# A decoder layer in float32: the sums of eight weight blocks and one rstd product, moved in the order of the instructions

## The chip, the cores and the metric

The kernel runs on one core of one Trainium2 chip. The core has five engines that run beside each other and are tied by semaphores: TensorE (PE in the profile, its weight loads are PEld), VectorE (DVE), ScalarE (ACT), GpSimd (POOL) and SyncE (SP). Here POOL and SP do little but issue transfers. Each engine works through its own instructions in one order that is fixed when the kernel is built. The metric is the device time of one execution in microseconds (us); lower is better.

## The reference

One layer of a hybrid decoder on 256 tokens of 2048 features, all in float32. What is computed:

```
h = rms_norm(x, g_mix);  z = h @ w_in
y = concat(pool_mixer(z_pool), mla(z_q, z_kv, z_kr), memory_attention(z_mq, mem)) @ w_o
x = x + y
h2 = rms_norm(x, g_ffn)
g = h2 @ w_gate;  gc = conv_b + conv_w[0]*g[t-2] + conv_w[1]*g[t-1] + conv_w[2]*g[t]
x = x + (silu(gc) * (h2 @ w_up)) @ w_down
```

The feed-forward width is 5632, so w_gate and w_up are cut into 44 tiles of 128 columns each, and w_down into 44 rows of blocks, taken in pairs.

## The kernel before, in words

**Products.** Each float32 weight block comes from memory into a staging tile `wr` (8 KB for each of 128 partitions, three buffers). ScalarE rounds half of it to a high part `wh` (line 102), VectorE subtracts to get the low part `wl` (line 103); each has four buffers. TensorE then makes three products: high by high, high by low, low by high. The out-projection takes its activations as the stationary operand (`gemm_n`, lines 184 to 186, 512 columns, results in `psm`); the first gate and up tile use `gemm_t` (line 133), the other 43 use `gemm_pair` (line 168).

**The out-projection** is 16 calls of `out_part`, counted from 0. The first eight take the activations of the pooling and memory branches (`catm`, part of `cat`), with the steps of the eight attention heads between their products; the last eight take those of the MLA heads, two for each of the four column blocks n. One part loads one block of `w_o` and splits it in two halves of 12 products each. After the second part of a column block `out_add` (line 804) adds the product to `x1n`, ScalarE squares it (line 830) and POOL stores it to `x1s` (line 831). `turn(n)` transposes a finished block on TensorE (line 837) and splits the result into `h2`, tile `h`: ScalarE makes the high half (line 196), VectorE the low half (line 197). In the stream of TensorE `turn(n - 1)` stands behind the two parts of block n, so `turn(2)` stands at the end of the out-projection.

**The jobs.** The down-projection at the end of the layer saves products by working on differences of weight blocks. For some block rows those differences are made far ahead and parked in memory: a job loads one block row of `w_down` into a tile `wk` (`job_load`, line 757, on POOL's queue), makes four differences in place (`job_sums`, line 764, VectorE) and writes them to `tsum` in two stores (line 766, POOL's queue). The first eight jobs run during the out-projection with two buffers for `wk`; the others run in the feed-forward stage with tiles `wj`. `first_jobs`, called at the end of each part, runs the next job if the part's number is in the table `FIRST` (line 768), and then starts the load for the job after the next, into the buffer that has just been stored. So a load waits until both stores of the job two before it have landed.

**The first gate tile** is begun early: `gemm_t` on features 0 to 1023 for gate and up (line 913), then `turn(3)` for the last column block, then `x1_rstd` (line 915), then `gemm_t` on features 1024 to 2047 for gate and up (line 919). `x1_rstd` sums the squares, takes the root on ScalarE (line 211), inverts it on VectorE, makes two diagonal matrices `tok` (line 857) and multiplies them by a matrix of ones (line 859), so that `r1` holds the rstd of each token on all partitions (copy on line 860, ScalarE). `r1` is first needed by `glu(0)` (line 871), which runs in the middle of gate tile 1. Block 3 of `h2` is needed by the last four of the eight k steps of the second half.

**What sets the order.** The kernel is written as one program; a scheduler spreads it over the engines by its own costs. `keep` marks instructions that are to be taken in the order of the program; the others may be moved more freely. The products of the parts numbered over 8 and the splits are not marked. The order that comes out is the one that counts; it is shown below where the change touches it.

Of the kernel before, what the change touches and what calls it, by code (L numbers as in the profile page):

```python
# [22 lines left out]
KD = D // P  # L23
# [14 lines left out]
HS = 1024  # L38
# [26 lines left out]
def layer(ctx, tc, xT_d, xn_d, memT_d, vec_d, tab_d, w_z_d, w_mqkr_d, w_q_d, w_kv_d, w_mem_d, w_pool_d, w_o_d,  # L65
# [14 lines left out]
    def ps_main():  # L80
        return psm.tile([P, 512], F32, tag="m", name=nm("psm"))

    def ps_aux():
        return psa.tile([P, 512], F32, tag="a", name=nm("psa"))

    def load_w(src, n, cut=STG, kept=False):
        raw = stage.tile([P, STG], F32, tag="wr", name=nm("wr"), bufs=3)
        for c in range(0, n, cut):
            keep(nc.sync.dma_start(raw[:, c:min(n, c + cut)], src[:, c:min(n, c + cut)]), kept)
        return raw[:]  # L90
# [5 lines left out]
    def split_w(raw, o, n, cut=HS, kept=False, shift=0):  # L96

        hi = stage.tile([P, HS + 64], F32R, tag="wh", name=nm("wh"), bufs=4)[:, shift:shift + HS]
        lo = stage.tile([P, HS + 64], F32R, tag="wl", name=nm("wl"), bufs=4)[:, shift:shift + HS]
        for c in range(0, n, cut):  # L100
            e = min(n, c + cut)
            keep(nc.scalar.copy(hi[:, c:e], raw[:, o + c:o + e]), kept)  # L102
            keep(nc.vector.tensor_tensor(lo[:, c:e], raw[:, o + c:o + e], hi[:, c:e].bitcast(F32), op=ALU.subtract),  # L103
                 kept)
        return hi, lo
# [7 lines left out]
    def rounds(act, k, low):  # L113

        m = act(k)
        h, l = (m[:, 0], m[:, 1]) if len(m.shape) == 3 else (m[:, 0:T], m[:, T:2 * T])
        return (h,) if low else (h, l)

    def gemm_t(ps, raw, o, act, ks, first=True, last=True, between=None):


        ks = list(ks)
        nk = HS // P
        cs = range(0, len(ks), nk)
        for c in cs:
            kc = ks[c:c + nk]

            parts = split_w(raw, o + c * P, len(kc) * P, shift=16 if c // nk % 2 else 48)
            lows = (False, True) if c // nk % 2 == 0 else (True, False)
            for low in lows:  # L130
                for i, k in enumerate(kc):
                    for a, m in enumerate(rounds(act, k, low)):
                        nc.tensor.matmul(ps, parts[low][:, i * P:(i + 1) * P], m,  # L133
                                         start=first and c + i + a == 0 and not low,
                                         stop=last and c == cs[-1] and i == len(kc) - 1 and low == lows[1],
                                         skip_group_check=True)
            if between is not None and c == 0:
                between()
# [70 lines left out]
    def rsqrt_(dst, src, scale):  # L209

        nc.scalar.activation(dst, src, AF.Sqrt, bias=eps[:], scale=scale)
        nc.vector.reciprocal(dst, dst)
# [22 lines left out]
    def tok():  # L235
        return mp.tile([P, 512], F32, tag="tok", name=nm("tok"), bufs=3)
# [79 lines left out]
    ps = ps_aux()  # L316
# [24 lines left out]
    pss = [[ps_main()[:] for _ in range(2)] for _ in range(NT)]  # L341
    for c in range(KD // 2):
        raw = raw0 if c == 0 else load_w(w_mem_d[c], STG, HS if c == 1 else STG)
# [16 lines left out]
    ps = ps_aux()  # L360
# [61 lines left out]
    pss = [[ps_aux()[:, :NH] for _ in range(2)] for _ in range(NT)]  # L422
    for c in range(KD // 2):
        raw = load_w(w_mqkr_d[c], 2 * 576)
# [41 lines left out]
    class Head:  # L466
# [23 lines left out]
        def turn(self):  # L490
            tp = ps_aux()
            for x, (k, i) in enumerate(self.blocks):
                a = self.spans[i][0]
                keep(nc.tensor.transpose(tp[:, x * P:(x + 1) * P], self.p[:, a + k * P:a + (k + 1) * P], identf[:]))
            self.pT = mp.tile([P, 512], F32, tag="pT", name=nm("pT"), bufs=2)
            nb = len(self.blocks) * P
            nc.scalar.copy(self.pT[:, :nb], tp[:, :nb])
# [37 lines left out]
    for m in range(6):  # L535
        raw = load_w(w_z_d[m], STG)
        if m in (1, 3):
            keep(nc.sync.dma_start(x1n[:, m // 2, :], xn_d[m // 2]))
        ps = ps_main()[:, 0:T]
# [212 lines left out]
    def job_place():  # L752
        return fp.tile([P, STG], F32, tag="wj", name=nm("wj"), bufs=2)[:]

    def job_load(i, raw):

        keep(nc.gpsimd.dma_start(raw, w_dn_d[SUMMED[i]]))
        return i, raw

    def job_sums(i, raw):  # L760

        r = raw.rearrange("p (b n) -> p b n", n=NN)
        for d, a, b in ((1, 0, 1), (0, 2, 0), (2, 2, 1), (3, 3, 2)):
            keep(nc.vector.tensor_tensor(r[:, d], r[:, a], r[:, b], op=ALU.subtract))  # L764
        for h in range(2):
            keep(nc.gpsimd.dma_start(tsum[:, i, h * HS:(h + 1) * HS], raw[:, h * HS:(h + 1) * HS]))  # L766

    FIRST = (1, 2, 4, 6, 8, 9, 11, 13)

    def first_load(i):  # L770
        return job_load(i, mp.tile([P, STG], F32, tag=("xgt", "zl")[i % 2], name=nm("wk"))[:])
# [4 lines left out]
    def first_jobs():  # L776

        if parts[0] in FIRST:
            i, raw = waiting.pop(0)
            job_sums(i, raw)  # L780
            if i + 2 < len(FIRST):
                waiting.append(first_load(i + 2))
# [23 lines left out]
    pss = {}  # L806
# [33 lines left out]
    for n in range(4):  # L840
        pss = [[ps_main()[:]] for _ in range(NT)]
# [10 lines left out]
    def x1_rstd():  # L852
        nc.vector.tensor_reduce(rc[:], ssx[:], axis=AX.X, op=ALU.add)
        rsqrt_(rc[:], rc[:], 1.0 / D)
        dg = tok()
        for tt in range(NT):
            nc.vector.tensor_scalar(dg[:, tt * P:(tt + 1) * P], identf[:], rc[:, tt:tt + 1], None, op0=ALU.mult)
        ps = ps_aux()
        nc.tensor.matmul(ps[:, 0:T], ones[:], dg[:, 0:T], start=True, stop=True)
        nc.scalar.copy(r1[:], ps[:, 0:T])  # L860
# [49 lines left out]
    raws = [load_w(w[0], STG) for w in (w_g_d, w_u_d)]  # L910
    pss = [ps_main()[:, 0:T] for _ in range(2)]
    for ps, raw in zip(pss, raws):
        gemm_t(ps, raw, 0, h2, range(8), last=False)
    turn(3)
    x1_rstd()
    mix.close()
    fp = ctx.enter_context(tc.tile_pool(name="ffn", bufs=1))
    for ps, raw in zip(pss, raws):
        gemm_t(ps, raw, HS, h2, range(8, KD), first=False)
    job = job_load(len(FIRST), job_place())  # L920
    late = len(SUMMED) - len(FIRST)
    job_at = {1 + i * (KF - 7) // (late - 1): len(FIRST) + i for i in range(late)}
    for f in range(1, KF):
        rows = [load_w(w[f], STG, kept=True) for w in (w_g_d, w_u_d)]
        behind = (lambda p=pss: glu(0, *p)) if f == 1 else None
        pss = [ps_main()[:, 0:T] for _ in range(2)]
# [220 lines left out]
```

## Time and profile before

| | |
|---|---|
| three runs | 996.36, 997.23 and 997.76 us; median 997.23 us |
| the profiled execution | 996.85 us, of which 995.1 us lie between its first and last instruction (the span) |
| busy: PE, PEld, DVE, ACT, POOL | 986.6, 912.9, 784.1, 577.7, 67.1 us |
| granted TensorE clock | 0.999 of full speed |
| transfers | 294.88 MB, 296 GB/s on average |

In the rows below a line of the timeline reads: start in us from the beginning of the span, length in us, engine, line of the kernel, operation, tile written <- tiles read, how many, and in brackets how long the engine stood before it and what released it. Several instructions of one kind in a row are merged into one line. Numbers at the end of a tile's name are left out in the profile, and stand in the order of the instructions.

### The profile page before, as it was taken

The page shows a single profiled execution, that of the slowest core. Times are in us where ns is not written, and L with a number is a line of the kernel's source. Part 1 is how long each engine was busy: PE and PEld are TensorE (multiplying, and loading weights), DVE is VectorE, ACT ScalarE, POOL GpSimd, SP SyncE. Part 2 cuts the span into 40 slices and gives each one's busy share as a digit, 9 for nine tenths or more (in the row PEclk, how much of TensorE's full clock was granted, in tenths as well). Part 3 has the DMA queues.
Part 4 walks back from the last instruction along what each step waited for, and adds up shares of the span by engine and source line. Part 5 has one row for each costly group of instructions (what it writes and reads, how often), then busy time and mean ns, then how long its engine had stood idle before and what let it go on. Part 6 is the DMA issues. An engine that isn't in the chain of part 4 may idle for free.

```text
span 995.1 us, 17312 instructions
## 1 busy us (share of the span) xinstructions
PE 986.6 (99%) x6870; PEld 912.9 (92%) x6870; DVE 784.1 (79%) x1174; ACT 577.7 (58%) x779; POOL 67.1 (7%) x130
## 2 busy tenths in 40 slices
PE   9999999999999999999999999999999999999998
PEld 8899988888879999999999999999999888888886
DVE  6878588977677788767868877777876889899987
ACT  6777665644466555455555545555454666847763
POOL 1100000110210101000000100000000000000000
PEclk9999999999999999999999999999999999999999
DMA  9867446696798977888877788879897999999992
GB/s 360 295 244 287 137 160 221 233 323 239 295 323 316 349 283 273 310 291 294 292 298 275 276 293 312 307 264 333 307 354 259 343 396 356 370 340 391 368 388 100
DMA packets 50577, 294.88 MB, mean 296 GB/s; under 512 B 5696, under 2 KB 6208, under 8 KB 25024
## 3 DMA queue, kind: packets, MB, share of 16 engines
q1 hardware_dynamic: 33696, 213.16, 58.8%
q0 software_dynamic: 16368, 79.83, 21.5%
q8 instruction: 54, 0.88, 0.3%
q10 hardware_dynamic: 432, 0.79, 0.2%
q14 instruction: 27, 0.22, 0.1%
HBM read 255.61 MB, written 38.14 MB: 295 GB/s over the span
## 4 chain that ended last, share of the span: by engine, by line
PE 94%; DVE 2%; DMA 1%; ACT 1%; issue 1%; POOL 0%; DVEq 0%; POOLq 0%
PE psm L168 47%; PE psm L184 4%; PE psm L185 4%; PE psm L186 4%; PE psm L149 4%; PE psa L958 4%; PE psa L957 4%; PE psa L956 4%; PE psm L958 4%; PE psm L957 4%; PE psm L956 4%; PE psm L133 2%; PE psa L722 1%; DMA wk<-in_w_dn 1%; PE psa L184 1%; PE psa L186 1%
## 5 line engine op out<-in xcount | busy, mean ns | idle before, releaser
L103 DVE TENSOR_TENSOR wl<-wr,wh 128x1024 fp32r<-128x1024 f32 (+2 forms) x344 | 397.1, 1162 | 135.7 <-ACT wh L102 121.8
L102 ACT CAST wh<-wr 128x1024 fp32r<-128x1024 f32 (+2 forms) x344 | 343.0, 1002 | 183.8 <-PE psm L168 87.5
L168 PE MATMUL psm<-h,wh 128*128 128x256 f32 x2752 | 319.1, 276 | 0.0
L168 PEld LDWEIGHTS psm<-h,wh 128*128 128x128 f32 x2752 | 315.3, 188 | 0.0
L168 PE MATMUL psm<-h,wl 128*128 128x256 f32 x1376 | 162.9, 276 | 0.0
L168 PEld LDWEIGHTS psm<-h,wl 128*128 128x128 f32 x1376 | 159.2, 188 | 0.0
L873 ACT ACTIVATE gc<-g,vec 128x256 f32<-128x256 f32 x44 | 26.5, 603 | 73.0 <-DVE g L871 73.0
L102 ACT CAST wh<-wj 128x1024 fp32r<-128x1024 f32 (+1 forms) x48 | 47.1, 982 | 22.0 <-PE psa L957 11.6
L103 DVE TENSOR_TENSOR wl<-wj,wh 128x1024 fp32r<-128x1024 f32 (+1 forms) x48 | 53.7, 1132 | 6.3 <-ACT wh L102 2.4
L764 DVE TENSOR_TENSOR wj<-wj 128x512 f32<-128x512 f32 x80 | 55.0, 687 | 1.0
L876 ACT ACTIVATE gc<-gc 128x256 f32<-128x256 f32 x44 | 18.4, 417 | 59.6 <-DVE gc L875 59.6
L875 DVE SCALAR_TENSOR_TENSOR gc<-g,vec,gc 128x255 f32<-128x255 f32 x88 | 42.3, 481 | 1.5
L103 DVE TENSOR_TENSOR wl<-dn,wh 128x1024 fp32r<-128x1024 f32 (+1 forms) x36 | 40.1, 1133 | 3.4 <-ACT wh L102 1.7
L102 ACT CAST wh<-dn 128x1024 fp32r<-128x1024 f32 (+1 forms) x36 | 35.4, 983 | 10.7 <-PE psm L957 4.9
L186 PE MATMUL psm<-wl,cat 128*128 128x512 f32 x96 | 37.6, 391 | 1.5 <-DVE wl L103 1.5
L766 POOL DMA_DIRECT2D tsum<-wj x40 | 21.4, 534 | 257.9 <-DVE s L896 166.1
L184 PE MATMUL psm<-wh,cat 128*128 128x512 f32 x96 | 38.1, 397 | 0.0
L185 PE MATMUL psm<-wh,cat 128*128 128x512 f32 x96 | 37.4, 389 | 0.0
L957 PE MATMUL psm<-wh,aS 128*128 128x512 f32 x84 | 32.7, 389 | 0.0
L957 PE MATMUL psa<-wh,aS 128*128 128x512 f32 x84 | 32.7, 389 | 0.0
L956 PE MATMUL psm<-wh,aS 128*128 128x512 f32 x84 | 32.7, 389 | 0.0
L956 PE MATMUL psa<-wh,aS 128*128 128x512 f32 x84 | 32.7, 389 | 0.0
(251 smaller groups left out, 1486.4 us busy)
## 6 DMA issues: line engine op xcount, KB each, us to landing
wr<-in_w_g SPq DMA_DIRECT2D x44, 1024.0 KB, 6.4
wr<-in_w_u SPq DMA_DIRECT2D x44, 1024.0 KB, 6.2
wj<-in_w_dn POOLq DMA_DIRECT2D x20, 1024.0 KB, 5.8
tsum<-wj POOLq DMA_DIRECT2D x40, 512.0 KB, 6.7
wr<-in_w_o SPq DMA_DIRECT2D x16, 1024.0 KB, 5.5
wr<-in_w_dn SPq DMA_DIRECT2D x16, 768.0 KB, 6.6
wr<-tsum SPq DMA_DIRECT2D x12, 1024.0 KB, 6.8
wj<-tsum SPq DMA_DIRECT2D x12, 1024.0 KB, 7.0
```

The lines of the kernel that those rows point to most:

```text
L102: keep(nc.scalar.copy(hi[:, c:e], raw[:, o + c:o + e]), kept)
L103: keep(nc.vector.tensor_tensor(lo[:, c:e], raw[:, o + c:o + e], hi[:, c:e].bitcast(F32), op=ALU.subtract), kept)
L149: keep(nc.tensor.matmul(ps, parts[k // nk][low][:, i * P:(i + 1) * P], m, start=k + a == 0 and low == low_first, stop=k == KD - 1 and low ...
L168: nc.tensor.matmul(ps, parts[k // nk][low][:, i * P:(i + 1) * P], m, start=k + a == 0 and low == (s == 1), stop=k == KD - 1 and low == (s ...
L184: keep(nc.tensor.matmul(ps, xh, hi[:, i, o], start=first and i == 0, stop=False), kept)
L185: keep(nc.tensor.matmul(ps, xl, hi[:, i, o], start=False, stop=False), kept)
L186: keep(nc.tensor.matmul(ps, xh, lo[:, i, o], start=False, stop=last and i == nk - 1), kept)
L764: keep(nc.vector.tensor_tensor(r[:, d], r[:, a], r[:, b], op=ALU.subtract))
L875: nc.vector.scalar_tensor_tensor(gc[:, d:T], g[:, 0:T - d], v(w, f), gc[:, d:T], op0=ALU.mult, op1=ALU.add)
L956: nc.tensor.matmul(ps, a[0], b[0], start=first, stop=False)
L957: nc.tensor.matmul(ps, a[1], b[0], start=False, stop=False)
L958: nc.tensor.matmul(ps, a[0], b[1], start=False, stop=last)
```

## The change

Two edits. The table of the parts behind which the eight jobs' sums run is another one, and in the first gate tile `x1_rstd` moves from ahead of the second half of gate and up to the place between them. `mix.close()` and the opening of the next pool, which free and take the memory of the tiles of the first stages, come after these products instead of ahead of them. No instruction is added or taken away.

```diff
-    FIRST = (1, 2, 4, 6, 8, 9, 11, 13)
+    FIRST = (1, 3, 4, 6, 7, 9, 10, 12)
...
     turn(3)
-    x1_rstd()
+    for i, (ps, raw) in enumerate(zip(pss, raws)):
+        gemm_t(ps, raw, HS, h2, range(8, KD), first=False)
+        if i == 0:
+            x1_rstd()
     mix.close()
     fp = ctx.enter_context(tc.tile_pool(name="ffn", bufs=1))
-    for ps, raw in zip(pss, raws):
-        gemm_t(ps, raw, HS, h2, range(8, KD), first=False)
```

The second job runs one part later; the fifth, seventh and eighth run one part earlier. Three places show what this makes of the order.

POOL's queue from the load for the fifth job (`wk_2398`) on; the load for the seventh is `wk_2645` before and `wk_2587` after, the load for the eighth is `wk_2687` in both. Before:

```order
L757 DMA wk_2398<-in_w_dn 128x2048
L766 DMA tsum<-wk_2260 128x1024 x2
L757 DMA wk_2534<-in_w_dn 128x2048
L766 DMA tsum<-wk_2398 128x1024 x2
L831 DMA x1s<-x1n 128x512 x2
L757 DMA wk_2645<-in_w_dn 128x2048
L766 DMA tsum<-wk_2534 128x1024 x2
L766 DMA tsum<-wk_2645 128x1024
L757 DMA wk_2687<-in_w_dn 128x2048
```

The same queue after:

```order
L757 DMA wk_2398<-in_w_dn 128x2048
L766 DMA tsum<-wk_2324 128x1024 x2
L757 DMA wk_2534<-in_w_dn 128x2048
L766 DMA tsum<-wk_2398 128x1024 x2
L757 DMA wk_2587<-in_w_dn 128x2048
L766 DMA tsum<-wk_2534 128x1024 x2
L757 DMA wk_2687<-in_w_dn 128x2048
L831 DMA x1s<-x1n 128x512 x2
L766 DMA tsum<-wk_2587 128x1024 x2
```

The last two loads have moved ahead: the seventh job's is no longer behind stores of `x1s`, the eighth job's stands ahead of the first of them. On VectorE, before, the sums of the sixth job (`wk_2534`, behind the splits of part 9) stand ahead of those of the fifth (`wk_2398`, behind the splits of part 10); after, those of the fifth begin just ahead of the splits of part 8, and those of the sixth keep their place.

VectorE in parts 12 and 13, where the sums are those of the seventh job before and of the eighth after; `wl_2840` and `wl_2856` before, `wl_2846` and `wl_2862` after, are the splits for the two halves of part 13. Before:

```order
L103 TENSOR_TENSOR wl_2822<-wr_2803,wh_2821 128x1024
L764 TENSOR_TENSOR wk_2645<-wk_2645 128x512
L103 TENSOR_TENSOR wl_2840<-wr_2837,wh_2839 128x1024
L764 TENSOR_TENSOR wk_2645<-wk_2645 128x512
L804 TENSOR_TENSOR x1n<-x1n,psm_2697 128x512
L764 TENSOR_TENSOR wk_2645<-wk_2645 128x512
L804 TENSOR_TENSOR x1n<-x1n,psm_2698 128x512
L764 TENSOR_TENSOR wk_2645<-wk_2645 128x512
L197 SCALAR_TENSOR_TENSOR h_2584<-psa_2781,vec,h_2584 128x256
L197 SCALAR_TENSOR_TENSOR h_2584<-psa_2786,vec,h_2584 128x256
L197 SCALAR_TENSOR_TENSOR h_2584<-psa_2791,vec,h_2584 128x256
L197 SCALAR_TENSOR_TENSOR h_2584<-psa_2796,vec,h_2584 128x256
```

After:

```order
L103 TENSOR_TENSOR wl_2822<-wr_2803,wh_2821 128x1024
L764 TENSOR_TENSOR wk_2687<-wk_2687 128x512 x3
L103 TENSOR_TENSOR wl_2846<-wr_2843,wh_2845 128x1024
L804 TENSOR_TENSOR x1n<-x1n,psm_2697 128x512
L804 TENSOR_TENSOR x1n<-x1n,psm_2698 128x512
L764 TENSOR_TENSOR wk_2687<-wk_2687 128x512
L103 TENSOR_TENSOR wl_2862<-wr_2843,wh_2861 128x1024
L197 SCALAR_TENSOR_TENSOR h_2592<-psa_2781,vec,h_2592 128x256
```

Before, the split `wl_2856` follows the four instructions on `h`; after, `wl_2862` stands ahead of them. The sums behind which the splits of parts 14 and 15 stood (job eight before) are gone from there.

TensorE in the second half of the first gate tile, from `turn(3)` on; `wh_3101`, `wl_3102` and `wh_3088`, `wl_3089` are the gate's weights, `psm_3011` is up. Before:

```order
L837 MATMUL psa_3083<-identf,x1n 128x128 x2
L133 MATMUL psm_3010<-h_2584,wh_3101 128x256 x4
L859 MATMUL psa_3094<-tok_3091,ones 128x256
L133 MATMUL psm_3010<-h_2584,wh_3101 128x256 x4
L133 MATMUL psm_3010<-h_2585,wh_3101 128x256 x8
L133 MATMUL psm_3010<-h_2584,wl_3102 128x256 x4
```

After:

```order
L837 MATMUL psa_3083<-identf,x1n 128x128 x2
L133 MATMUL psm_3010<-h_2592,wh_3088 128x256 x8
L133 MATMUL psm_3010<-h_2593,wh_3088 128x256 x8
L133 MATMUL psm_3010<-h_2592,wl_3089 128x256 x4
L133 MATMUL psm_3010<-h_2593,wl_3089 128x256 x4
L859 MATMUL psa_3122<-tok_3119,ones 128x256
L133 MATMUL psm_3011<-h_2592,wh_3125 128x256 x8
```

The rstd's product (line 859) stood behind four of the gate's 24 products; it now stands behind all 24, ahead of the 24 of up. `h_2585` and `h_2593` are block 3 of `h2`, made from `turn(3)`.

## Prediction

> **What bounds the kernel now.** First the page: the span and the busy times.
>
> ```profile
> span 995.1 us, 17312 instructions
> PE 986.6 (99%) x6870; PEld 912.9 (92%) x6870; DVE 784.1 (79%) x1174; ACT 577.7 (58%) x779; POOL 67.1 (7%) x130
> ```
>
> TensorE is the bound, and it works 986.6 of 995.1 us. An edit that only moves instructions can win back idle time of TensorE alone. So the second view is the busy time by stretch, one that ends with the out-projection and the first gate tile, and one that is the feed-forward stage behind it.
>
> ```profile
> 160.00:300.00 140.00, 137.26 (x716) 116.00 (x716) 108.72 (x198) 75.19 (x138) 17.16 (x32) 1.00 0.78 280
> 300.00:725.00 425.00, 425.00 (x3749) 424.97 (x3749) 327.59 (x477) 221.79 (x262) 33.67 (x63) 1.00 0.83 299
> ```
>
> (Columns: length, busy PE, PEld, DVE, ACT, POOL, granted clock, share of the DMA engines, GB/s.) In the stretch of the change TensorE stands 140.00 − 137.26 = 2.74 us. In the next one it never stands, so what is won before 300 is carried on: a TensorE that arrives earlier there moves everything behind it. The third view is TensorE's timeline in the first stretch, and it has two stops, whose bracketed times, 1.52 and 1.21, make up the 2.74. The first is in part 13 of the out-projection:
>
> ```profile
> 273.67 0.39 PE L184 MATMUL psm<-wh,cat 128*128 128x512 f32 x1
> 273.89 0.39 PE L185 MATMUL psm<-wh,cat 128*128 128x512 f32 x1
> 275.81 0.50 PE L186 MATMUL psm<-wl,cat 128*128 128x512 f32 x1 [1.52 <-DVE wl L103]
> 276.15 0.40 PE L184 MATMUL psm<-wh,cat 128*128 128x512 f32 x1
> ```
>
> Products start every 0.22 to 0.23 us, so the one at 275.81 was due at 274.12: 1.69 us lost by starts, and 0.11 more because the next comes 0.34 behind it. It waits for the second split of that part. VectorE's timeline shows why that is late:
>
> ```profile
> 260.28 1.23 DVE L103 TENSOR_TENSOR wl<-wr,wh 128x1024 fp32r<-128x1024 f32 x1 [1.50 <-ACT wh L102]
> 268.22 0.69 DVE L764 TENSOR_TENSOR wk<-wk 128x512 f32<-128x512 f32 x1 [6.71 <-DMA wk<-in_w_dn]
> 268.83 1.22 DVE L103 TENSOR_TENSOR wl<-wr,wh 128x1024 fp32r<-128x1024 f32 x1
> 272.97 1.65 DVE L197 SCALAR_TENSOR_TENSOR h<-psa,vec,h 128x256 fp32r<-128x256 f32 x4
> 274.54 2.35 DVE L103 TENSOR_TENSOR wl<-wr,wh 128x1024 fp32r<-128x1024 f32 x2
> ```
>
> The seventh job's first sum stands for 6.71 us until its load has landed, and all splits stand behind it. TensorE lost only 1.69 of these: the split buffers covered the other 5.0. POOL's queue shows why the load came late:
>
> ```profile
> 251.84 0.53 POOL L766 DMA_DIRECT2D tsum<-wk  x1 [19.24 <-DVE wk L764]
> 254.29 0.53 POOL L766 DMA_DIRECT2D tsum<-wk  x1 [1.92 <-DVE wk L764]
> 255.73 0.55 POOL L831 DMA_DIRECT2D x1s<-x1n  x1 [0.30 <-issue]
> 258.46 0.54 POOL L757 DMA_DIRECT2D wk<-in_w_dn  x1 [2.18 <-DMA tsum<-wk]
> ```
>
> POOL stood 19.24 us for the fifth job's sums, and the load, issued at 258.46, needed that job's stores. On VectorE the sums of the sixth job came first and those of the fifth after them:
>
> ```profile
> 243.38 2.13 DVE L764 TENSOR_TENSOR wk<-wk 128x512 f32<-128x512 f32 x3
> 245.77 0.68 DVE L764 TENSOR_TENSOR wk<-wk 128x512 f32<-128x512 f32 x1
> 250.12 2.14 DVE L764 TENSOR_TENSOR wk<-wk 128x512 f32<-128x512 f32 x3
> ```
>
> The second stop is in the first gate tile, at the rstd's product:
>
> ```profile
> 290.84 2.13 PE L133 MATMUL psm<-h,wh 128*128 128x256 f32 x16
> 293.75 2.05 PE L133 MATMUL psm<-h,wh 128*128 128x256 f32 x16
> 296.58 1.25 PE L837 MATMUL psa<-identf,x1n 128*128 128x128 f32 x8
> 297.58 0.71 PE L133 MATMUL psm<-h,wh 128*128 128x256 f32 x4
> 299.51 0.70 PE L859 MATMUL psa<-tok,ones 128*128 128x256 f32 x2 [1.21 <-DVE h L197]
> ```
>
> From 290.84 to 293.75 are 24 products (16 and the 8 of the low part): 0.121 each. The four at 297.58 are through at 298.06, so by starts 299.51 − 298.06 = 1.45 are lost. The product needs `tok` and a free `psa` bank; both come from VectorE, where the chain of the rstd and block 3 of `h` is late:
>
> ```profile
> 290.90 2.36 DVE L103 TENSOR_TENSOR wl<-wr,wh 128x1024 fp32r<-128x1024 f32 x2 [1.53 <-PE psa L837]
> 293.18 1.28 DVE L804 TENSOR_TENSOR x1n<-x1n,psm 128x512 f32<-128x512 f32 x2
> 298.98 1.65 DVE L197 SCALAR_TENSOR_TENSOR h<-psa,vec,h 128x256 fp32r<-128x256 f32 x4
> ```
>
> ScalarE, on which that chain runs for most of its way:
>
> ```profile
> 289.82 2.95 ACT L102 CAST wh<-wr 128x1024 fp32r<-128x1024 f32 x3 [1.71 <-DMA wr<-in_w_u]
> 293.90 0.63 ACT L830 ACTIVATE tok<-x1n 128x512 f32<-128x512 f32 x1 [1.13 <-DVE x1n L804]
> 295.19 1.55 ACT L196 ACTIVATE h<-psa,vec 128x256 fp32r<-128x256 f32 x4
> 298.25 1.55 ACT L196 ACTIVATE h<-psa,vec 128x256 fp32r<-128x256 f32 x4
> 300.25 0.37 ACT L860 COPY r<-psa 128x256 f32<-128x256 f32 x1 [0.44 <-PE psa L859]
> 300.59 2.00 ACT L102 CAST wh<-wr 128x1024 fp32r<-128x1024 f32 x2
> ```
>
> The last additions to `x1n` could have begun when the last part's products ended, about a microsecond of transposes before 290.84, near 290.2. They began at 293.18, behind casts that waited for the first up block and splits that waited for the casts. That block was issued late because its buffer was held by a split in part 14, which stood behind the eighth job's sum, which again waited for a load:
>
> ```profile
> 278.80 0.69 DVE L764 TENSOR_TENSOR wk<-wk 128x512 f32<-128x512 f32 x1 [1.92 <-DMA wk<-in_w_dn]
> 280.66 0.33 SPq L89 DMA_DIRECT2D wr<-in_w_u  x1
> ```
>
> So both stops go back to the jobs' place in the order.
>
> **The change part by part.** Nothing is added or removed: 32 sums, 16 stores, 8 loads and one small product are the same. What counts is where they stand.
>
> *The jobs.* The fifth job's sums now stand ahead of the sixth's, two parts earlier, so the 19.24 us stand of POOL goes. The sixth job's sums keep their place (243.38, the fourth ending at 246.5), and the eighth job's load needs only its stores. How long that takes I bound by the transfers of lines 766 and 757:
>
> ```profile
> DMA to landing us min/median/max: 2.9/6.9/12.3
> DMA to landing us min/median/max: 4.9/6.0/10.7
> ```
>
> (First the stores, then the loads.) 246.5 + 6.9 + 6.0 = 259.4; at worst 246.5 + 12.3 + 10.7 = 269.5. The sums that stand in part 12 are now this job's. VectorE reaches them when the split at 260.28 ends, at 261.4. When must the load have landed? From a landing at L the new order takes three sums (0.61 each, 268.83 − 268.22), a split (1.14 to the next), two additions and a sum (0.6 each) and the split itself (1.22): L + 6.0. TensorE wants it at 274.12, so L may be 268.1. Half a part earlier the same reckoning gives 268.3. The middle estimate has 8.7 us in hand, and even the old landing at 268.2 would now cost 0.1, because the four instructions at 272.97 no longer stand ahead of the split. I take the whole gap: 1.69 + 0.11 = **1.8 us** won (bounds: 0.4 for the worst landing, 1.8).
>
> The second job, one part later, delays its stores and so the load of the fourth job's data.
>
> ```profile
> 204.05 1.22 DVE L103 TENSOR_TENSOR wl<-wr,wh 128x1024 fp32r<-128x1024 f32 x1
> 220.97 2.14 DVE L764 TENSOR_TENSOR wk<-wk 128x512 f32<-128x512 f32 x3
> ```
>
> In the new order its sums are done ahead of the split at 204.05; 204.05 + 6.9 + 6.0 = 217.0, ahead of the place at 220.97 where the data is used. At worst it is 227.1, a stand of 6.1, of which 5.0 are covered as above: 1.1 us lost at the bound. I take nothing. POOL's later stores of `x1s` are wanted only at the end of the layer.
>
> *The rstd's product.* Alone it would help like this: TensorE goes on with eight products instead of four and the first on block 3's high half, to 297.58 + 9 × 0.121 = 298.67; the next needs the first low half, which is there at 298.98 + 0.42 = 299.40, and by the distance seen before it (299.51) TensorE starts 0.84 late in place of 1.45. That wins 0.6, the lower bound. With the jobs out of the way the upper bound comes in reach: the wait at 278.80 is gone, so the up block is issued well before 280.66 and the casts no longer wait 1.71 for it; the additions follow the last part directly, at 290.2 in place of 293.18. Then the squares and the first four instructions on `h` end at about 296.74 − 2.9 = 293.8, and block 3 is limited by its transposes alone: the first pair is out a quarter of their 1.0 us after 296.58, ScalarE then needs 0.4 and VectorE 0.4 for each, so the first low half is there at 297.7 and the fourth at about 299, where TensorE wants them at 298.7 and 297.58 + 15 × 0.121 = 299.4. It fits with 0.4 to hand. I take **1.3 us** of the 1.45.
>
> What now stands behind the product: ScalarE's copy to `r1` and, behind it in its order, the casts of gate tile 1. From the end of the product they take 0.34 + 1.0 = 1.4 us (300.25 to 300.59, then half of 2.00), while TensorE has 24 products of up, 2.9 us, to do. The cover is 1.5 us; were it gone, each microsecond the cast is late would cost one. `glu(0)` wants `r1` later still. The first load for a `wj` tile, which waits for the freed memory, moves by about as much and is used a whole gate tile later.
>
> The sum: 1.8 + 1.3 = 3.1 us. The span goes from 995.1 to 992.0 and the profiled execution from 996.85 to 993.75. That execution lies 0.38 under the median of the runs; from the median it would be 994.1. I say **994.0 us**, 0.32% less.
>
> [...]
>
> **The rivals.**
>
> *Half of the second stop stays* (994.7 us, 0.12). The up block lands late though it is issued early, since the DMA engines are 78% busy over this stretch; then only 0.6 of the second term is won: 997.1 − 2.4. Against it speaks that the block has some 7 us more.
>
> *The stop in part 13 only moves* (996.5 us, 0.10): another late load meets another sum, and only the 0.6 remains. For it speaks that both late waits came from one chain on POOL's queue, which still alternates stores and loads over two buffers; against it the margins of 8.7 and 4 us.
>
> *Slower: the eighth load lands late* (999.6 us, 0.04). Place: VectorE's first sum in part 12. From a landing at 268.1 each microsecond costs one. At 269.9 the gain of the first term is used up; the up block is then late again, so with the 0.6 the kernel is slower than before from 270.5 on. A landing at 273 costs 4.9 against 2.4 won: +2.5. The worst sum of the rows is 269.5, which is why the chance is small. [...] Here the stops of 1.5 and 1.2 left the granted clock at 1.00, and no run shows a longer one.
>
> *The edit of the rstd costs what it wins* (995.6 us, 0.04): the copy to `r1` holds up the casts of gate tile 1 beyond its cover, and the second term is lost.
>
> **How the numbers follow.** The forecast has 0.70, with a range of its own of 993.0 to 995.0: the runs before spread from 996.36 to 997.76, and the terms give 2.4 to 3.45. About what a measurement of this kernel can tell is 0.2%, 2.0 us, so "faster" is under 995.2. The forecast gives 0.69 of that, the first rival 0.09: 0.78. The second and the fourth and the rest of the first are within 0.2%: 0.18. Slower: 0.04. The range that leaves out two in ten reaches to the second rival without its upper half: 992.8 to 996.3.
>
> **What the new profile would show.** Right: no idle time of PE by line 186 in part 13 and at most 0.3 us between `turn(3)` and the end of up; PE busy in the stretch 160 to 297 within 0.5 us of its length; POOL without a stand of 19 us, and the load that serves part 12 issued near 253 and landed by 262; the up block issued before 276, no wait of ACT for it; line 804 of the last block within half a microsecond of the last part's products. Wrong: a wait of VectorE's line 764 for a load of more than 5 us, a stop of PE at the first product of gate tile 1 behind ACT's line 102, or a stop of PE at line 133 for VectorE's line 197 of more than 0.8 us.

## The result, and the profile after

The changed kernel takes 993.87 us (median of seven runs, 993.72 to 994.27) against 997.23 us (seven runs beside them, 995.87 to 997.76): a ratio of 0.9969 taken over all these runs (the two medians alone give 0.9966), with a 95% interval from 0.9958 to 0.998. Its profiled execution took 994.18 us with a span of 992.4 us; that of the kernel before took 996.85 and 995.1 us.

First the page, then the busy time by stretch, of the changed kernel (columns as in the prediction):

```profile
span 992.4 us, 17314 instructions
PE 986.3 (99%) x6870; PEld 913.5 (92%) x6870; DVE 784.3 (79%) x1174; ACT 578.0 (58%) x779; POOL 66.8 (7%) x130
```

```profile
160.00:300.00 140.00, 140.00 (x744) 119.59 (x744) 109.82 (x199) 76.16 (x140) 17.20 (x33) 1.00 0.79 286
300.00:725.00 425.00, 425.00 (x3748) 425.00 (x3747) 329.09 (x478) 222.07 (x264) 33.45 (x63) 1.00 0.84 300
```

TensorE works as long as before (986.3 us against 986.6). The page counts two instructions more than before; they are not among those that it counts as busy work of an engine, whose numbers are the same. The 2.74 us that it stood between 160 and 300 us are gone: 140.00 busy of 140.00.

POOL's timeline of the changed kernel, where the stand of 19.24 us was:

```profile
234.49 0.53 POOL L766 DMA_DIRECT2D tsum<-wk  x1 [2.56 <-DVE wk L764]
242.71 0.54 POOL L757 DMA_DIRECT2D wk<-in_w_dn  x1 [7.70 <-DMA tsum<-wk]
246.91 0.53 POOL L766 DMA_DIRECT2D tsum<-wk  x1 [1.13 <-DVE wk L764]
256.15 0.53 POOL L757 DMA_DIRECT2D wk<-in_w_dn  x1 [8.71 <-DMA tsum<-wk]
```

The seventh job's load is issued at 242.71 us where it was 258.46, the eighth's at 256.15 where it was 272.43. VectorE's timeline shows what is left of the wait that stopped TensorE in part 13:

```profile
260.45 1.23 DVE L103 TENSOR_TENSOR wl<-wr,wh 128x1024 fp32r<-128x1024 f32 x1 [1.50 <-ACT wh L102]
264.26 2.14 DVE L764 TENSOR_TENSOR wk<-wk 128x512 f32<-128x512 f32 x3 [2.58 <-DMA wk<-in_w_dn]
266.32 1.22 DVE L103 TENSOR_TENSOR wl<-wr,wh 128x1024 fp32r<-128x1024 f32 x1
```

VectorE stands 2.58 us in place of 6.71, and the split behind it is done at 267.5. TensorE's timeline around the first gate tile, to be read against the prediction's rows of the same lines:

```profile
294.87 1.04 PE L837 MATMUL psa<-identf,x1n 128*128 128x128 f32 x8
295.66 2.23 PE L133 MATMUL psm<-h,wh 128*128 128x256 f32 x16
298.64 0.59 PE L859 MATMUL psa<-tok,ones 128*128 128x256 f32 x2
298.88 2.23 PE L133 MATMUL psm<-h,wh 128*128 128x256 f32 x16
301.90 3.93 PE L168 MATMUL psm<-h,wh 128*128 128x256 f32 x32
316.78 3.79 PE L168 MATMUL psm<-h,wl 128*128 128x256 f32 x32
```

No bracket stands in it: nothing is waited for. Gate tile 1 (line 168) starts at 301.90; in the trace of before it did at 305.23:

```profile
305.23 2.04 PE L168 MATMUL psm<-h,wh 128*128 128x256 f32 x16
319.82 3.79 PE L168 MATMUL psm<-h,wl 128*128 128x256 f32 x32
989.57 2.37 SPq L1031 DMA_DIRECT2D out_t<-dn  x4
990.41 0.39 PE L958 MATMUL psm<-wl,aT 128*128 128x512 f32 x1
```

The last two rows are the end of before. The changed kernel's end (its lines there are one higher):

```profile
986.53 2.38 SPq L1032 DMA_DIRECT2D out_t<-dn  x4
987.37 0.39 PE L959 MATMUL psm<-wl,aT 128*128 128x512 f32 x1
```

Last product and last stores are both 3.04 us earlier, 0.29 less than gate tile 1. These 0.29 us go where TensorE never stands: from the start of gate tile 1 to the last row of line 168 shown, in gate tile 2, it is 14.88 us (301.90 to 316.78) where it was 14.59 (305.23 to 319.82), with the products a little farther apart. The span is shorter by 2.7 only: the four last stores took 2.8 us from issue to landing (median) where they took 2.2 before. The medians lie 3.36 us apart. That is more than either trace difference, and the section on the experiments comes back to it.

### The profile page after: what moved, and what is told of

It reads as the page before. It is cut to its first block, busy times and chain, and to the rows that moved or that the text cites. A ratio compares the mean times of both kernels' runs of the same rounds, so it can differ in the third digit from the quotient of the medians.

```text
span 992.4 us, 17314 instructions
## 1 busy us (share of the span) xinstructions
PE 986.3 (99%) x6870; PEld 913.5 (92%) x6870; DVE 784.3 (79%) x1174; ACT 578.0 (58%) x779; POOL 66.8 (7%) x130
## 4 chain that ended last, share of the span: by engine, by line
PE 98%; DVE 1%; ACT 0%; issue 0%
PE psm L168 47%; PE psm L184 5%; PE psm L185 5%; PE psm L186 5%; PE psm L149 4%; PE psa L959 4%; PE psa L958 4%; PE psm L959 4%; PE psa L957 4%; PE psm L958 4%; PE psm L957 4%; PE psm L133 2%; PE psa L722 1%; PE psa L184 1%; PE psa L186 1%; PE psa L185 1%
```

## The experiments

The theory: both stops of TensorE come from one thing, the fifth job's sums standing late on VectorE, behind the sixth's, while POOL waits for them with the seventh's load behind it. The rival: the edits each take their own stop, 1.8 us and 1.3 us, and add up. The first four kernels (the fifth job alone and back, the jobs and the rstd alone) ran beside 22 runs of the kernel before (median 997.25 us), the next four beside 21 more (median 997.36 us), one of which took 5711.34 us and is left out of the ratios.

**The fifth job alone.** The kernel before, with one number changed:

```diff
-    FIRST = (1, 2, 4, 6, 8, 9, 11, 13)
+    FIRST = (1, 2, 4, 6, 7, 9, 11, 13)
```

> The kernel before with the fifth job alone put a part earlier (parts 1, 2, 4, 6, 7, 9, 11, 13 in place of 1, 2, 4, 6, 8, 9, 11, 13); the rstd's product in its old place. Theory: GpSimd's stand of 19 us is the fifth job's sums standing in its queue ahead of the seventh's load; with the fifth job alone moved, that load is issued near 242 us in place of 258, and the eighth's near 256, so both stops of TensorE go or shrink to some tenths: 2.3 to 2.9 us won, 994.3 to 994.9 us. Rival (each job stands too late by itself, so that the seventh and eighth have to be moved for the gain): the stops stay at 1.3 us or more each, and less than 0.6 us is won, 996.6 us or above.

993.79 us (993.40 to 993.96), ratio 0.9965, interval 0.9952 to 0.9977: the whole gain from one digit, and 0.5 us under the range of the theory. POOL's timeline of this kernel:

```profile
244.76 0.54 POOL L757 DMA_DIRECT2D wk<-in_w_dn  x1 [9.99 <-DMA tsum<-wk]
258.35 0.53 POOL L757 DMA_DIRECT2D wk<-in_w_dn  x1 [11.16 <-DMA tsum<-wk]
```

The second row is the eighth job's load; at about that time (258.46) the kernel before issued the seventh's. One whole job's delay has left the queue. TensorE works 45.00 of the 45.00 us from 255 to 300.

**The fifth job back.** The changed kernel, with that one job at its old place:

```diff
-    FIRST = (1, 3, 4, 6, 7, 9, 10, 12)
+    FIRST = (1, 3, 4, 6, 8, 9, 10, 12)
```

> The changed kernel with the fifth job alone put back behind part 8 (parts 1, 3, 4, 6, 8, 9, 10, 12). Theory: GpSimd stands again for some 15 to 19 us, the load of the job behind part 10 is issued near 258 us, and since its sums stand a part earlier than in the kernel before, VectorE waits for it at least as long as there: the first stop is back with 1.5 us or more, up to 5 us, 995.5 to 999 us. Rival (the early places of the last three jobs are what counts): within 0.5 us of the changed kernel's 993.9 us.

997.06 us (996.15 to 998.17), ratio 1.0001, interval 0.9993 to 1.001: the whole gain is gone, though the second, seventh and eighth jobs and the rstd's product stand as in the changed kernel. POOL's timeline, then the list of TensorE's waits (engine, line, what it waited for, us in total, times, longest):

```profile
252.16 0.53 POOL L766 DMA_DIRECT2D tsum<-wk  x1 [19.77 <-DVE wk L764]
259.03 0.54 POOL L757 DMA_DIRECT2D wk<-in_w_dn  x1 [2.44 <-DMA tsum<-wk]
```

```profile
PE psm L186 <- DVE wl L103: 1.5, 1, 1.5
PE psm L133 <- DVE h L197: 0.3, 1, 0.3
```

The stand of POOL is back with 19.77 us, and the stop in part 13 with 1.5. The fifth job's place is necessary and, by the run above, enough.

**The jobs without the rstd, and the rstd without the jobs.** The first is the kernel before with the new table alone, the second the changed kernel with the old table:

```diff
-    FIRST = (1, 2, 4, 6, 8, 9, 11, 13)
+    FIRST = (1, 3, 4, 6, 7, 9, 10, 12)
```

> The kernel before with the new places of the eight jobs alone; the rstd's product stands behind the second half of the up tile as before. Theory: both long stops of TensorE are worked by the late loads, so the stop in part 13 (1.69 us) is gone, and the stop ahead of the rstd's product shrinks from 1.45 us by starts to 0.2 us or less, since the up tile's block is loaded some 6 us earlier: 2.9 us won, some 994.3 us. Rival (the two parts of the change add up, each taking its own stop): only the first stop goes, 1.8 us won, some 995.4 us, and the trace still shows about 1.3 us of idle TensorE ahead of the rstd's product.

994.24 us (993.80 to 994.40), ratio 0.9968, interval 0.9956 to 0.998.

```diff
-    FIRST = (1, 3, 4, 6, 7, 9, 10, 12)
+    FIRST = (1, 2, 4, 6, 8, 9, 11, 13)
```

> The kernel before with the rstd's product moved alone; the jobs stand in their old places. Theory: the stop in part 13 stays at 1.5 to 1.7 us, and of the second stop about 0.8 us stays, now on the up tile's late block, so 0.6 us is won, some 996.6 us. Rival (the two parts add up): the second stop goes whole, 1.3 us won, some 995.9 us. If the first stop's length is what scatters the times of the kernel before (some 1.9 us from the shortest run to the longest), this kernel's scatter like them, and those of the kernel with the new places for the jobs stay within 0.6 us.

997.23 us (995.24 to 998.58), ratio 0.9999, interval 0.999 to 1.0008. The interval reaches from 1.0 us won to 0.8 lost: the theory's 0.6 lies in it, the rival's 1.3 does not. TensorE's timeline of the jobs alone and then of the rstd alone:

```profile
294.72 1.03 PE L837 MATMUL psa<-identf,x1n 128*128 128x128 f32 x8
295.51 0.71 PE L133 MATMUL psm<-h,wh 128*128 128x256 f32 x4
296.18 0.70 PE L859 MATMUL psa<-tok,ones 128*128 128x256 f32 x2
301.90 3.93 PE L168 MATMUL psm<-h,wh 128*128 128x256 f32 x32
```

```profile
296.52 1.04 PE L837 MATMUL psa<-identf,x1n 128*128 128x128 f32 x8
297.31 2.98 PE L133 MATMUL psm<-h,wh 128*128 128x256 f32 x16
304.33 2.87 PE L168 MATMUL psm<-h,wh 128*128 128x256 f32 x23
```

From the last transposes (line 837) to gate tile 1 (line 168) it is 8.65 us before, 7.03 in the changed kernel, 7.18 with the jobs alone and 7.81 with the rstd alone. So the second stop was 1.62 us; the jobs alone take away 1.47 of it, the rstd's move alone 0.84. The 0.78 that stay in the last case are hidden inside a merged row: 16 products of line 133 take 2.98 us where the changed kernel needs 2.23. The two edits do not add up; they take the same stop, and the jobs take nearly all of it. The runs scatter as the theory had it: over 3.3 us with the rstd alone, over 0.6 with the jobs alone.

**The smallest version.** The fifth job alone, and the rstd's product moved:

```diff
-    FIRST = (1, 3, 4, 6, 7, 9, 10, 12)
+    FIRST = (1, 2, 4, 6, 7, 9, 11, 13)
```

> The kernel before with the fifth job alone a part earlier and the rstd's product moved: the smallest version of the whole change. Theory: with the late loads gone, the rstd's product in its old place cost only some 0.15 us (product to gate tile by starts 7.18 us against 7.03), so this is 0.1 us or so faster than the fifth job alone, 993.4 to 993.9 us, the same as the changed kernel. Rival (the rstd's move is worth its own 1.3 us whatever the loads do): 992.5 us.

993.75 us (993.25 to 993.93), ratio 0.9963, interval 0.9949 to 0.9977: the same as the fifth job alone (993.79) and as the changed kernel (993.87). From the transposes to gate tile 1 it takes 7.06 us. With the loads on time the rstd's move is worth 0.12 us in the trace and nothing that the runs can tell.

**The second job back.** The changed kernel with:

```diff
-    FIRST = (1, 3, 4, 6, 7, 9, 10, 12)
+    FIRST = (1, 2, 4, 6, 7, 9, 10, 12)
```

> The changed kernel with the second job alone put back behind part 2 (parts 1, 2, 4, 6, 7, 9, 10, 12). Theory: the later place of the second job neither costs nor wins, since the third and fourth jobs' loads land ahead of their sums either way: 993.9 us, within 0.3 us. Rival (the change's later second job was needed to make room for the third or cost something by making the fourth later): more than 0.5 us to either side, with a stop of TensorE between 190 and 230 us where it costs.

994.10 us (994.00 to 994.31): the second job's place is worth nothing that these runs show, as forecast. VectorE's timeline of this kernel:

```profile
254.92 2.14 DVE L764 TENSOR_TENSOR wk<-wk 128x512 f32<-128x512 f32 x3 [4.77 <-DMA wk<-in_w_dn]
266.36 2.15 DVE L764 TENSOR_TENSOR wk<-wk 128x512 f32<-128x512 f32 x3 [2.86 <-DMA wk<-in_w_dn]
```

Here the seventh job's data came 4.77 us after VectorE was ready for it, and the eighth's as late as 266.36 us; TensorE worked 45.00 of 45.00 us all the same.

**The cover of a stand.** The changed kernel with the eighth job's sums one part earlier, so that VectorE reaches them sooner than their data can be there:

```diff
-    FIRST = (1, 3, 4, 6, 7, 9, 10, 12)
+    FIRST = (1, 3, 4, 6, 7, 9, 10, 11)
```

> The changed kernel with the eighth job's sums one part earlier still (parts 1, 3, 4, 6, 7, 9, 10, 11): they stand ahead of the splits of part 12 in VectorE's queue, which reaches them near 256.5 us, while their data lands near 264.2 us as in the changed kernel: a stand of some 7.7 us. Theory: part 12's first split then ends at 264.2 + 1.4 + 1.2 = 266.8 us, TensorE wants it at about 265.6 us, so it stands for 1.2 us (0.8 to 2): some 995.1 us, and the runs scatter more. Rival (a stand of VectorE costs TensorE nothing as long as the buffers split ahead last): no stop, 993.9 us. Rival (the whole stand, less the 5.0 us of cover seen in part 13 of the kernel before): 2.7 us, 996.6 us.

994.69 us (993.75 to 997.69), ratio 0.9976, interval 0.9967 to 0.9984, and two more traces of it:

> The kernel with the eighth job's sums one part earlier still, for another trace of it. Its 11 runs lie between 993.75 and 997.69 us; in the profiled one, 994.11 us, the data landed at 261.2 us and TensorE had no stop. Theory: where the run takes over 994.7 us, the eighth job's data lands later than 263 us and TensorE stops in part 12, by 1 us for each us of the landing behind about 263.0 us. Rival (the scatter is not from this load): a slow run shows no stop in part 12.

> The same kernel a third time, with the same expectations: a stop in part 12 by what the eighth job's data lands behind about 263.0 us, or, by the rival, none whatever the time.

993.55 and 994.19 us. VectorE's timeline in the third of the three traces:

```profile
261.37 1.42 DVE L764 TENSOR_TENSOR wk<-wk 128x512 f32<-128x512 f32 x2 [5.02 <-DMA wk<-in_w_dn]
```

The data landed near 261 us in all three (260.94, 261.17, 261.37), three microseconds ahead of what was expected, and the stand was 4.68 to 5.02 us in place of 7.7. TensorE had no stop for it. So the price of a longer stand wasn't measured: what these traces show is that 5 us cost nothing. The expected scatter came, with 996.38 and 997.69 us among the 11 runs, but none of the three traces fell on such a run. That those two stopped in part 12 is argued, not shown; the one of 997.69 us has a mean granted clock of 0.998, the other of 1.000.

**The cover of the copy.** The changed kernel with the rstd's product directly ahead of gate tile 1:

```diff
-    for i, (ps, raw) in enumerate(zip(pss, raws)):
+    for ps, raw in zip(pss, raws):
         gemm_t(ps, raw, HS, h2, range(8, KD), first=False)
-        if i == 0:
-            x1_rstd()
+    x1_rstd()
```

> The changed kernel with the rstd's product behind the second halves of both tiles, directly ahead of the first gate tile of the loop. Theory: ScalarE's copy of the product and the casts that stand behind it in its queue were covered by the up tile's second half; without that cover the first matmul of the gate tile waits for product, copy and first cast, 0.6 + 0.4 + 1.0 us from the product's start less the 0.24 us that TensorE works on: a stop of about 1.4 us, 995.3 us. Rival (the casts of that gate tile are early anyway): no stop, 993.9 us.

995.96 us (995.60 to 996.28), ratio 0.9988, interval 0.998 to 0.9997. TensorE's and ScalarE's timelines:

```profile
301.12 0.59 PE L859 MATMUL psa<-tok,ones 128*128 128x256 f32 x2
303.12 4.03 PE L168 MATMUL psm<-h,wh 128*128 128x256 f32 x32 [1.41 <-ACT wh L102]
```

```profile
301.75 0.37 ACT L860 COPY r<-psa 128x256 f32<-128x256 f32 x1 [5.28 <-PE psa L859]
302.01 2.94 ACT L102 CAST wh<-wr 128x1024 fp32r<-128x1024 f32 x3
```

The stop is 1.41 us, for 1.4 expected: product, copy and first cast in a row, with nothing of TensorE's beside them. The runs are slower by 1.9 than the one above with the second job back, which ran on the same chip; of its last products the trace shows 1.75 (988.69 against 986.94). The 0.34 beyond the stop lie in gate tiles 1 and 2: from the start of gate tile 1 to the same row of line 168 it is 14.98 us here (303.12 to 318.10) and 14.58 with the second job back (301.71 to 316.29). They do not belong to the edit. The same kernel shows both lengths: of the three traces with the eighth job's sums one part earlier, the first has 14.58 us (301.89 to 316.47) and the third 14.88 (301.72 to 316.60). What makes the difference stays open.

**The kernel before, twice more.** Before's runs scatter over 2 us and more, the changed kernel's over 0.55. Two more traces of the unchanged kernel should tell where that comes from.

> The kernel before once more, for another trace of it. Theory: its runs lie 2 us apart because the seventh and eighth jobs' loads land now earlier, now later, and TensorE's two stops are long by what they are late; the start of the first gate tile of the loop (305.23 us in the first trace, 301.7 to 301.9 us in every kernel without stops) moves with the run's time, by 0.8 us or more for each us of the time. Rival (the scatter comes from elsewhere, the end of the span or the rounds of transfers in the feed-forward part): the gate tile starts within 0.3 us of 305.2 us whatever the run takes.

> The kernel before a third time, with the same expectations: by the theory the gate tile's start follows the run's time, by the rival it stays within 0.3 us of 305.2 us.

996.05 and 997.44 us. TensorE's timeline of the one and of the other:

```profile
275.93 0.50 PE L186 MATMUL psm<-wl,cat 128*128 128x512 f32 x1 [1.75 <-DVE wl L103]
298.69 0.70 PE L859 MATMUL psa<-tok,ones 128*128 128x256 f32 x2 [0.55 <-DVE h L197]
304.41 2.85 PE L168 MATMUL psm<-h,wh 128*128 128x256 f32 x23
```

```profile
276.37 0.50 PE L186 MATMUL psm<-wl,cat 128*128 128x512 f32 x1 [2.01 <-DVE wl L103]
277.72 0.63 PE L184 MATMUL psm<-wh,cat 128*128 128x512 f32 x1
278.14 0.63 PE L185 MATMUL psm<-wh,cat 128*128 128x512 f32 x1
300.11 0.70 PE L859 MATMUL psa<-tok,ones 128*128 128x256 f32 x2
305.83 1.34 PE L168 MATMUL psm<-h,wh 128*128 128x256 f32 x10
```

Over the three traces of the kernel before gate tile 1 starts at 304.41, 305.23 and 305.83 us for times of 996.05, 996.85 and 997.44: 1.42 us of start for 1.39 us of time. So in these three executions the scatter of the kernel before arises ahead of gate tile 1, as the theory had it. How it arises is more than late landings. Between the executions of 996.05 and 996.85 us it is the up block, which lands 0.8 us apart (ScalarE starts its casts at 289.01 and 289.82). In that of 997.44 us the first stop is 2.01 us long, and behind it products start every 0.43 us in place of 0.23: the clock has fallen. The window view of that execution (length, busy PE, granted clock, DMA share, GB/s):

```profile
276.00:277.00 1.00, 0.63 (x3) 1.00 0.79 221
277.00:278.00 1.00, 1.00 (x4) 0.51 1.03 352
279.00:280.00 1.00, 1.00 (x4) 0.50 1.07 438
280.00:281.00 1.00, 1.00 (x8) 0.79 1.07 406
281.00:282.00 1.00, 1.00 (x8) 1.00 0.98 401
```

Half a clock for about 3.4 us (0.79 in the last partial slice is 0.4 us more at a half). From the product at 276.37 to the first one behind the transposes of block 2, at 281.15, it is 4.78 us, where the execution of 996.85 us has 3.22 (275.81 to 279.03): 1.56 us lost beyond the stop itself. TensorE is then so late that the second stop vanishes (7.18 us from transposes to gate tile).

The five traces with the first stop give its price. VectorE's stand ahead of the job's sum and TensorE's stop behind it, in us:

| kernel | stand of VectorE | stop of TensorE | difference |
|---|---|---|---|
| fifth job back | 6.68 | 1.49 | 5.19 |
| before | 6.71 | 1.52 | 5.19 |
| rstd alone | 6.89 | 1.70 | 5.19 |
| before, 996.05 us | 6.95 | 1.75 | 5.20 |
| before, 997.44 us | 7.20 | 2.01 | 5.19 |

Between stands of 6.68 and 7.20 us each tenth of a microsecond of the stand is a tenth of TensorE's; what a fallen clock adds comes on top. The stands of 4.68 to 5.02 us, ahead of earlier parts, lie under 5.19 and cost nothing.

## Why the prediction was right

*That TensorE's idle time is all there is to win, and that it carries through.* Right, but for 0.29 us: 3.33 us earlier at gate tile 1, 3.04 us at the last product, with no idle time in between. The difference lies in the pace of the products in gate tiles 1 and 2, which varies so between traces of one kernel.

*The first term, 1.8 us.* Right: the stop in part 13 is gone, and it went for the reason given, since the fifth job's place alone brings it back (1.5 us) or takes it away.

*The margin behind it.* Mis-sized. The prediction reckoned 246.5 + 6.9 + 6.0 = 259.4 us for the eighth job's landing, 8.7 us ahead of its limit of 268.1, with the load issued near 253. It was issued at 256.15 and landed at 264.26: POOL stood 8.71 us for the stores, and the load took 8.1. In hand were 3.8 us. Over the four traces that have the fifth job's new place and the eighth's sums behind part 12 the landing lay between 263.34 and 266.36 us. The term that was too small is that of the stores: in five traces with the fifth job's new place (the changed kernel, the fifth job alone, the jobs alone, and the second and third trace with the eighth job's sums one part earlier) POOL stood 8.33 to 11.68 us for them ahead of this load, against the median of 6.9. The load's 6.0 was about right: in the four of these where VectorE stands for this load, so that its landing can be read, it took 5.7 to 5.8 us three times and 8.1 once. POOL's window view of the changed kernel (length, busy POOL, granted clock, DMA share, GB/s):

```profile
246.00:256.00 10.00, 0.53 (x1) 1.00 0.98 354
```

The DMA engines are busy 98% of the time while the stores are under way, against 81% over the span of the kernel before. That this made the stores slow is argued; no run changed it. The prediction's own worst case, 269.5, would have crossed the limit. The limit itself held as far as it was tried: 266.36 cost nothing.

*The 5.0 us that the split buffers cover.* Right: the prediction counts TensorE's loss by starts (6.71 − 1.69); by the bracketed stops of the table it is 5.19 us in five traces, with a price of one for one behind it. Stands of 4.68 to 5.02 us cost nothing in four others.

*The second job costs nothing.* Right: 994.10 us with it back.

*The second term, 1.3 us.* The size was a little small, and the reason given for it was only partly the right one. By starts the second stop was 1.62 us (the prediction counted 1.45 up to the rstd's product, without what the transposes lost), and all of it went. But the prediction put this term to the rstd's product, with the jobs as a help: 0.6 alone, up to 1.45 with them. The runs show the reverse. The jobs alone win 1.47, the rstd's move alone 0.84 in the trace and nothing in the runs, and on top of the jobs 0.12 to 0.15. The prediction had named the chain itself, from the eighth job's late load over the held buffer to the late up block, and this is what the jobs cut: the block is issued at 274.36 in place of 280.66 and ScalarE no longer waits for it. What it failed to do was to price the jobs without the rstd.

*The copy and the casts behind the rstd's product.* Right: covered where it stands, 1.41 us where it does not.

*The sum.* 3.1 us forecast, 3.04 to 3.33 on the engines, 2.7 in the span, 3.36 between the medians. The span fell short by the last stores' landing. The medians gained more than the traces; the first traced execution of before was one without the fallen clock, and with it gate tile 1 starts 4.0 us later than in the kernels without stops (305.83 against some 301.8). Of the 22 runs beside the first experiments, the 14 with a mean clock of 0.999 or 1.000 have a median of 996.66 us, 0.6 under that of all: without the rest the gain would be some 2.8 us, about that of the span. So it is in part luck that the median came within 0.13 us of the forecast: the second term won 0.3 us more than was taken and the fallen clock some 0.6, which the sum did not have; gate tiles 1 and 2 took back 0.29 and the end of the span 0.3. The upper bound that the prediction gives for its terms is a slip: 1.8 + 1.45 are 3.25, not 3.45.

*The rivals.* "The stop only moves" and "the eighth load lands late" both hung on the landing; the first did not come, and the second was nearer than its 0.04 said, with 3.8 us in hand instead of 8.7. "Half of the second stop stays" is what the rstd alone does, not the change. The copy to `r1` did not cost what the edit won; by the prediction's own terms that rival would have been 997.1 − 1.8, some 995.3 us and not 995.6.

## What to carry to other kernels

Where an in-order queue issues both the stores of one job and the load of another, look on it for the longest stand, and follow what the standing instruction waits for; one job's work at the wrong place in another engine's order delayed everything behind it, and moving that one job gave the gain of the whole edit. When two stops lie on one chain, price each edit with and without the other before adding. And do not take a landing for safe by the medians over the span: here the stores ahead of one load held it for 8.33 to 11.68 us in five traces, all above their median of 6.9.

## What the runs showed of the hardware

In one execution a stop of TensorE cost more than its length. After stops of 1.5 to 1.75 us the granted clock stayed at 1.00 in every trace; after one of 2.01 us it was 0.50 from about 277.0 to 280.4 us, which lost another 1.56 us. Nothing between 1.75 and 2.01 us was seen. What brings the clock down, and what sets how long it stays there, is not shown by these runs. The end of the span shows how far the fall varies. Behind the last product TensorE stands for good, and the clock falls there too: in the trace of before some 2.5 us after the end of that product (990.8 us; the clock is 0.63 from 993 to 994 us and 0.50 behind), in that of the changed kernel some 2.2 us after it (987.8 us; 0.99 from 989 to 990 us and 0.50 behind). Farther apart are the second job back, whose last product ends at about 987.3 us, and the rstd's product behind up, where it ends at about 989.1 (length, busy PE, granted clock, DMA share, GB/s):

```profile
989.00:990.00 1.00, 0.00 (x0) 0.66 0.99 375
993.00:994.00 1.00, 0.00 (x0) 1.00 0.00 0
```

In the first the clock is at a half from about 989.3 us, in the second still whole at 994.0. So by these traces the clock can be down after a stand of 2 us and still whole after one of nearly 5. The prediction had only stops of 1.5 and 1.2 us before it, both with a clock of 1.00 behind them, and gave a fall no part in its sum.

The runs without a trace fit. In the 44 runs of before, of the fifth job back and of the rstd alone that the first comparison holds, 14 have a mean granted clock of 0.998 or 0.997, and all 14 take over 997.0 us; the other 30 have 0.999 or 1.000 and lie between 995.24 and 998.17 us, so a fallen clock is not the only way to a long run. (The fall behind the last product is in these means too: the trace of before has 1.00 up to 900 us, 0.50 from 994 to 995 us and a mean of 0.999.) In the 28 runs of the five kernels that have the fifth job's new place and no stop, none is under 0.999, and all lie between 993.25 and 994.40 us. So the change took away the stops, and no run without them shows the lower mean clock; the forecast, made from one execution, had no such gain in its sum.

A load of 1 MB landed 8.1 us after its issue in one execution and 5.8 us after it in another, for the same job (issued 256.15, landed 264.26; issued 255.60, landed 261.37).
